# MLP of a two-layer decoder trunk: one buffer pool for both products, stepped weight loads, scratch split by group, last four groups by token tile

## The chip, the cores and the metric

One NeuronCore of a Trainium2 chip runs the whole program. The metric is the device time of one execution in microseconds (us); lower is better. Engines are named as in the profile: PE is TensorE, DVE VectorE, ACT ScalarE, POOL GpSimd, SP the engine whose queue issues nearly all DMAs.

## The reference, cut to what matters

Two layers over 1024 tokens of width 1024. Layer 0 mixes tokens with a causal pooling mixer, layer 1 with a gated DeltaNet; both then run the same MLP, whose two products are what the change is about (D = 1024, hidden width 4096):

```
x  = layer_norm(ALPHA * x + mix, ...)
ff = square(relu(x @ w1)) @ w2
pe = sigmoid(x @ gate_w + gate_b) * (p @ ple_proj)
x  = layer_norm(ALPHA * x + ff + pe, ...)
```

## The kernel before, in words

A float32 product is made of three float32r products: `split` (L66) rounds an operand to a high part (ACT copy, L68) and subtracts it for a low part (DVE, L69), and `mm3` (L71) issues high·high (L73), high·low (L74) and low·high (L75), each a 128x128 by 128x512 matmul.

Both MLP products are cut in 2x2 blocks and formed by seven block products instead of eight (P1 to P7, in the order P1, P2, P5, P6, P7, P4, P3 of the second product), whose operands are sums and differences of blocks. `mlp(i, ...)` (L306) runs once per layer i, in two stages:

**Stage A, h = square(relu(x @ w1))** (L325 to L419). The hidden width is taken in 16 pairs p of 128-column strips. A table `order` interleaves the products of pair p with the last two (P4, P3) of pair p-1, seven products of 12 matmuls a pair; `prep_a` prepares the weights three products ahead, from two loads of 512 KB into the three `raw` buffers. `multiply_a` evicts: the four blocks of h of the pair are c11, c12, c22, c21, and the combinations that the second product needs are hs2, hs3, hs4. All seven are 128x512 tiles from a pool `mlpa` of 10 buffers, made after P3 (L399 to L405: a DVE add, two ACT operations, four DVE operations) and stored by seven DMAs (L407) into one DRAM scratch tensor `h_d` for both layers.

**Stage B, ff = h @ w2** (L421 to L524). The pool of stage A is closed and a pool `mlpb` of five 128x2x512 buffers is opened. For each of seven products there are eight groups g; group g contracts over the strips of pairs 2g and 2g+1. `prep_b(k, g)` loads the left operand from `h_d` (L459, 512 KB into a `raw` buffer) and splits it into lh, ll (buffers `wh`, `wl` of a pool with two each); the right operand, a piece of w2, is split into rh, rl (pool `mlpb`). Sums of w2 blocks are formed in place by DVE (L323). `multiply_b` runs the group over four token tiles tt (24 matmuls a group, 192 a product, 1344 for all seven). w2 comes in 16 pieces of 1 MB through `load_w2` (L425): eight before the first group, eight when group 4 of P1 is reached (L507). The `big` pool of ten 16 KB-per-partition buffers holds them and, in stage A, the left operands r1.

The first four token tiles are normalised (`norm`, L495) after groups 1 to 4 of P3, one each; the last two groups of P3 run token tile by token tile, each followed by its `norm`. In layer 1 `layer_norm` (L101) writes the output by DMA (L126).

The order of instructions on each engine is fixed when the program is built, by a scheduler that places operations by readiness; within an engine, and on SP's queue, nothing overtakes. A tile that takes over a buffer waits for what last wrote or read it.

Of the kernel before, what the change touches and what calls it, by code (L numbers as in the profile page):

```python
# [7 lines left out]
F32 = mybir.dt.float32  # L8
# [24 lines left out]
def trunk(ctx: ExitStack, tc: tile.TileContext, io: dict):  # L33
# [272 lines left out]
    def mlp(i, r1, acc, row, finish=None, lag=0, out=None):  # L306
# [15 lines left out]
        stats = new_stats()  # L322
        sub = lambda o, a, b: V.tensor_tensor(o, a, b, ALU.subtract)  # L323
        add = lambda o, a, b: V.tensor_tensor(o, a, b, ALU.add)  # L324
        with tc.tile_pool(name=f"mlpa{i}", bufs=1) as q:  # L325
            new_h = lambda s: q.tile([P, 512], F32, tag="h", name=nm(s), bufs=10)
            st = {}
            n_op = [0]

# [34 lines left out]
            def multiply_a(p, k):  # L364
                d = st[p]
                o, ps, h = d["op"].pop(k), d["ps"], d["h"]
                bank = {P1: 0, P6: 0, P7: 0, P4: 0, P2: 1, P5: 2, P3: 2}[k]
                new = k in (P1, P2, P5)
                if new:
                    ps[bank] = new_ps()  # L370
                b = ps[bank]
                for kk in range(4):
                    mm3(b, o[:, 0, kk, :], o[:, 1, kk, :], r1[k][0][:, kk, :], r1[k][1][:, kk, :],
                        new and kk == 0, kk == 3, not new)

                def square(t):
                    A.activation(t, t, AF.Relu)
                    A.activation(t, t, AF.Square)

                if k == P1:  # L380
                    h[11] = new_h("c11")
                    A.copy(h[11], b)
                elif k == P2:
                    add(h[11], b, h[11])
                    square(h[11])
                elif k == P6:
                    h[12] = new_h("c12")
                    A.copy(h[12], b)
                elif k == P7:
                    h[22] = new_h("c22")  # L390
                    A.copy(h[22], b)
                    add(h[22], ps[2], h[22])
                    square(h[22])
                elif k == P4:
                    h[21] = new_h("c21")
                    A.activation(h[21], b, AF.Relu)
                    A.activation(h[21], h[21], AF.Square)
                elif k == P3:
                    add(h[12], b, h[12])  # L399
                    square(h[12])  # L400
                    s2, s3, s4 = (new_h(s) for s in ("hs2", "hs3", "hs4"))
                    sub(s3, h[12], h[11])
                    add(h[11], h[11], h[21])
                    sub(s2, h[11], h[12])
                    sub(s4, h[22], s2)  # L405
                    for n, t in ((P1, h[12]), (P2, h[22]), (P5, h[11]), (P6, s2), (P7, s3), (P4, h[21]), (P3, s4)):
                        nc.sync.dma_start(h_d[i, n, :, p, :], t)  # L407
                    del st[p]

            order = []  # L410
# [7 lines left out]
                    prep_a(*order[n + 3])  # L418
                multiply_a(*o)  # L419

        with tc.tile_pool(name=f"mlpb{i}", bufs=1) as q:  # L421
            new_op = lambda s, tag: (wsm if tag else q).tile([P, 2, 512], F32R, tag=tag or "op", name=nm(s), bufs=None if tag else 5)
            w = {}

            def load_w2(f, c):  # L425
                for e in range(2):
                    t = w[f, c, e] = new_big(F32, "w2").rearrange("p (g c) -> p g c", g=8)
                    src = io["w2"][i].rearrange("(g f p) c -> f p g c", f=2, p=P)
                    for b in range(2):
                        g = slice(e * 8 + b * 4, e * 8 + b * 4 + 4)  # L430
                        nc.sync.dma_start(t[:, b * 4:b * 4 + 4, :], src[f][:, g, cols(c)])

            def quad(f, c, g):
                return w[f, c, g // 4][:, g % 4 * 2:g % 4 * 2 + 2, :]

            ops = {}

            def prep_b(k, g):
                b11, b12, b21, b22 = ((f, c, 0) in w and quad(f, c, g) for f, c in ((0, 0), (0, 1), (1, 0), (1, 1)))
# [22 lines left out]
                split(rh, rl, r)  # L462
                ops[k, g] = lh, ll, rh, rl

            chain = {}
# [14 lines left out]
            def multiply_b(k, gs, tt):  # L480
                new = k in (P1, P2, P5)
                if new and gs[0] == 0:
                    chain[bank[k], tt] = new_ps()
                o = slice(tt * P, (tt + 1) * P)
                for g in gs:
                    lh, ll, rh, rl = ops[k, g]
                    for j in range(2):
                        mm3(chain[bank[k], tt], lh[:, j, o], ll[:, j, o], rh[:, j, :], rl[:, j, :],
                            new and g == 0 and j == 0, g == 7 and j == 1, not new)
                if gs[-1] == 7:  # L490
                    take(k, tt)
# [7 lines left out]
                if len(left) > lag:  # L499
                    left.pop(0)()  # L500

            load_w2(0, 0)
            load_w2(1, 0)
            seq = [(k, g) for k in (P1, P2, P5, P6, P7, P4, P3) for g in range(8)]
            prep_b(*seq[0])
            for n, (k, g) in enumerate(seq):
                if (k, g) == (P1, 4):  # L507
                    load_w2(0, 1)
                    load_w2(1, 1)
                if (k, g) == (P3, 0):  # L510
                    gb = new_big(F32, "gb")
                    g2, b2 = gb[:, 0:D], gb[:, D:2 * D]
# [1 line left out]
                    nc.sync.dma_start(b2, io["rows"][row + 4].partition_broadcast(P))  # L514
                if n + 1 < len(seq):
                    prep_b(*seq[n + 1])
                if (k, g) == (P3, 6):
                    continue
                for tt in range(4):
                    multiply_b(k, (6, 7) if (k, g) == (P3, 7) else (g,), tt)  # L520
                    if (k, g) == (P3, 7):
                        norm(4 + tt)
                if k == P3 and g in (1, 2, 3, 4):
                    norm(g - 1)  # L524
        return left

    x2_d = dram.tile([S, D], F32, name="x2_d")
# [706 lines left out]
```

## Time and profile before

| | |
|---|---|
| median of 3 runs | 2220.64 us (2218.31 to 2222.47) |
| the profiled execution's own time | 2214.46 us |
| its span, first to last instruction | 2212.7 us |
| mean granted TensorE clock | 0.985 |
| PE busy | 2136.8 us (97%), 10322 matmuls |
| DVE busy | 1523.7 us (69%) |
| ACT busy | 1058.6 us (48%) |
| DMA | 301.00 MB, mean 136 GB/s |

The page gives busy time by engine, the span in 40 slices, and the chain of work that ended last. The trace behind it can be asked for stretches of the span (`windows`), for single instructions in order of time (`timeline`) and for what each wait was ended by. In the timeline a row is: start in us, duration in us, engine, line, operation, tile written <- tiles read, shape, count, and in brackets the idle time of the engine just before, with what ended it. Tiles of one name in the program share a short name there: c11 to c22 are c, hs2 to hs4 are hs.

### The profile page before, as it was taken

To read this page: it belongs to the slowest core of one execution; us is meant where nothing else is said; L and a number is where in the kernel's file an instruction comes from. 1 tells how busy PE (TensorE), PEld (TensorE's weight loads), DVE (VectorE), ACT (ScalarE), POOL (GpSimd) and SP (SyncE) were. 2 spreads that over 40 slices of the span, in tenths; PEclk is the share of its full clock that TensorE was granted. 3 is DMA by queue.
4 is the path that set the end of the run, shared out by engine and by line. 5 is a ranking of instruction groups with operands and counts; after the bars stand their busy time and mean duration, and the time that the engine had idled before them with its cause. 6 is when DMAs were issued, how large, how long until landed. Compare 5 with 4: busy or idle time off the path is not lost.

```text
span 2212.7 us, 27931 instructions
## 1 busy us (share of the span) xinstructions
PE 2136.8 (97%) x10322; PEld 1784.3 (81%) x10322; DVE 1523.7 (69%) x2566; ACT 1058.6 (48%) x1814; POOL 24.4 (1%) x85
## 2 busy tenths in 40 slices
PE   7999999988999999999999999999999998899997
PEld 6887888866888878888887998888788887688886
DVE  7895666657674586879975677489666665657457
ACT  5434555543333456643455666343455554333334
POOL 0000000000000000000001000000000000000000
PEclk9999999998999999999999999999999999899999
DMA  8324445477333342341234445312444447733323
GB/s 297 110 81 138 153 157 153 146 246 262 102 114 96 96 144 84 92 128 48 91 129 127 117 129 183 122 35 84 135 157 149 149 149 245 270 96 115 98 92 124
DMA packets 158221, 301.00 MB, mean 136 GB/s; under 512 B 41410, under 2 KB 55106, under 8 KB 157764
## 3 DMA queue, kind: packets, MB, share of 16 engines
q1 hardware_dynamic: 153476, 290.82, 40.7%
q10 hardware_dynamic: 4608, 8.39, 1.0%
q8 instruction: 81, 1.33, 0.3%
q14 instruction: 56, 0.46, 0.1%
HBM read 208.99 MB, written 90.18 MB: 135 GB/s over the span
## 4 chain that ended last, share of the span: by engine, by line
PE 88%; DVE 6%; DMA 3%; ACT 2%; issue 1%; SPq 0%; DVEq 0%; ACTq 0%
PE ps L75 26%; PE ps L73 26%; PE ps L74 26%; DMA raw<-in_gate 1%; DVE w L323 1%; PE ps L134 1%; PE ps L772 1%; DMA raw<-in_w 1%; PE ps L746 1%; PE ps L1020 1%; PE ps L1042 1%; PE ps L984 1%; DMA stage<-in_pool_w 0%; PE ps L1008 0%; PE ps L1013 0%
## 5 line engine op out<-in xcount | busy, mean ns | idle before, releaser
L73 PE MATMUL ps<-rh,lh 128*128 128x512 f32 x896 | 351.9, 393 | 26.5 <-ACT rh L68 20.5
L75 PE MATMUL ps<-rh,ll 128*128 128x512 f32 x896 | 351.5, 392 | 9.0 <-DVE ll L69 9.0
L74 PE MATMUL ps<-rl,lh 128*128 128x512 f32 x896 | 351.3, 392 | 0.1
L69 DVE TENSOR_TENSOR rl<-w,rh 128x1024 fp32r<-128x1024 f32 x112 | 137.0, 1225 | 222.8 <-issue 174.3
L68 ACT CAST lh<-raw 128x1024 fp32r<-128x1024 f32 x112 | 118.1, 1055 | 353.6 <-PE ps L74 342.7
L73 PEld LDWEIGHTS ps<-rh,lh 128*128 128x128 f32 x896 | 169.7, 190 | 62.9 <-ACT rh L68 21.4
L75 PEld LDWEIGHTS ps<-rh,ll 128*128 128x128 f32 x896 | 169.8, 190 | 46.0 <-DVE ll L69 10.5
L73 PE MATMUL ps<-xh,wh 128*128 128x512 f32 x512 | 203.4, 397 | 1.2 <-ACT wh L68 1.2
L73 PE MATMUL ps<-xh,wo 128*128 128x512 f32 x512 | 200.3, 391 | 2.9 <-ACT wo L68 1.5
L75 PE MATMUL ps<-xh,wl 128*128 128x512 f32 x512 | 200.4, 391 | 1.1 <-DVE wl L69 1.1
L74 PE MATMUL ps<-xl,wh 128*128 128x512 f32 x512 | 200.1, 391 | 0.0
L74 PE MATMUL ps<-xl,wo 128*128 128x512 f32 x512 | 199.9, 390 | 0.0
L75 PE MATMUL ps<-xh,wo 128*128 128x512 f32 x512 | 199.8, 390 | 0.0
L74 PEld LDWEIGHTS ps<-rl,lh 128*128 128x128 f32 x896 | 169.8, 190 | 36.5 <-DVE rl L69 1.5
L69 DVE TENSOR_TENSOR wo<-raw,wo 128x512 fp32r<-128x512 f32 x192 | 132.3, 689 | 80.6 <-ACT wo L68 80.6
L68 ACT CAST wo<-raw 128x512 fp32r<-128x512 f32 x192 | 119.2, 621 | 104.4 <-PE ps L75 91.2
L73 PE MATMUL ps<-xt,wo 128*128 128x512 f32 x384 | 149.6, 390 | 2.1 <-ACT wo L68 2.1
L74 PE MATMUL ps<-xt,wo 128*128 128x512 f32 x384 | 149.4, 389 | 0.0
L75 PE MATMUL ps<-xt,wo 128*128 128x512 f32 x384 | 149.0, 389 | 0.0
L69 DVE TENSOR_TENSOR ll<-raw,lh 128x1024 fp32r<-128x1024 f32 x112 | 136.5, 1220 | 5.9 <-ACT lh L68 5.8
L68 ACT CAST rh<-w 128x1024 fp32r<-128x1024 f32 x112 | 116.8, 1046 | 30.3 <-PE ps L75 16.1
L324 DVE TENSOR_TENSOR c<-ps,c 128x512 f32<-128x512 f32 x96 | 66.1, 689 | 82.5 <-PE ps L75 73.9
(302 smaller groups left out, 4158.1 us busy)
## 6 DMA issues: line engine op xcount, KB each, us to landing
raw<-h_d SPq DMA_DIRECT2D x112, 512.0 KB, 3.5
raw<-in_w SPq DMA_DIRECT2D x64, 512.0 KB, 4.1
w<-in_w SPq DMA_DIRECT2D x32, 1024.0 KB, 8.2
h_d<-c SPq DMA_DIRECT2D x128, 256.0 KB, 2.1
h_d<-hs SPq DMA_DIRECT2D x96, 256.0 KB, 4.1
raw<-in_w_in SPq DMA_DIRECT2D x41, 512.0 KB, 3.5
pp_d<-tmp ACTq DMA_DIRECT2D x32, 256.0 KB, 3.1
raw<-in_gate SPq DMA_DIRECT2D x16, 512.0 KB, 4.9
```

What stands on the lines that cost most here:

```text
L68: A.copy(hi, src)
L69: V.tensor_tensor(lo, src, hi.bitcast(F32), ALU.subtract)
L73: T.matmul(ps, lh, rh, start=first, stop=False, skip_group_check=more)
L74: T.matmul(ps, lh, rl, start=False, stop=False, skip_group_check=more)
L75: T.matmul(ps, ll, rh, start=False, stop=last, skip_group_check=more)
L134: T.transpose(pss[q][:, j, :], y[:, k * P:(k + 1) * P], ident)
L323: sub = lambda o, a, b: V.tensor_tensor(o, a, b, ALU.subtract)
L324: add = lambda o, a, b: V.tensor_tensor(o, a, b, ALU.add)
L746: T.transpose(ps[:, j, :], chunk(tiles, half * 4 + j, h), ident)
L772: T.matmul(ps[:, j, :], kc, kc, start=True, stop=True)
L984: T.matmul(pq[:, j, :], hc("K", n, h), hc("Q", n, h), start=True, stop=True)
L1020: T.matmul(pv[:, j, :], d["X"][:, h, :], d["c"][:, 2 + gi, j], start=True, stop=True)
```

## The change

The seven single tiles of a pair become four paired ones ("c1" = c11 and c12, "c2" = c22 and c21, "hs23", and "hs4", of which half is used), from one pool `mlp` of five 128x2x512 buffers that stage B goes on using for rh and rl. The scratch is one DRAM tensor per layer and group of two pairs. A pair is stored by four DMAs (512, 512, 512 and 256 KB). The rl of the very first group of stage B is two single tiles from the pool `tmp`. `load_w2` loads one 1 MB piece a call: four before the first group, then one at every second group. The norms of the first four token tiles of P3 are asked for one group earlier in the code. In layer 1 (`out` is given) the last four groups of P3 run by token tile, with lh, ll, rh, rl in four `big` buffers; in layer 0 it stays at two groups.

```diff
-        with tc.tile_pool(name=f"mlpa{i}", bufs=1) as q:
-            new_h = lambda s: q.tile([P, 512], F32, tag="h", name=nm(s), bufs=10)
+        with tc.tile_pool(name=f"mlp{i}", bufs=5) as q:
+            new_h = lambda s: q.tile([P, 2, 512], F32, tag="q", name=nm(s))
+            place = {P5: 0, P1: 1, P2: 2, P4: 3, P6: 4, P7: 5, P3: 6}
...
-                    h[11] = new_h("c11")
+                    h[1] = new_h("c1")
+                    h[11], h[12] = h[1][:, 0], h[1][:, 1]
...
-                    h[22] = new_h("c22")
+                    h[2] = new_h("c2")
+                    h[22], h[21] = h[2][:, 0], h[2][:, 1]
...
-                    s2, s3, s4 = (new_h(s) for s in ("hs2", "hs3", "hs4"))
+                    d23, d4 = new_h("hs23"), new_h("hs4")
+                    s2, s3, s4 = d23[:, 0], d23[:, 1], d4[:, 0]
...
-                    for n, t in ((P1, h[12]), (P2, h[22]), (P5, h[11]), (P6, s2), (P7, s3), (P4, h[21]), (P3, s4)):
-                        nc.sync.dma_start(h_d[i, n, :, p, :], t)
+                    dst = h_d[i][p // 2][:, :, p % 2, :].rearrange("n p c -> p n c")
+                    nc.sync.dma_start(dst[:, 0:2], h[1])
+                    nc.sync.dma_start(dst[:, 2:4], h[2])
+                    nc.sync.dma_start(dst[:, 4:6], d23)
+                    nc.sync.dma_start(dst[:, 6], s4)
...
-        with tc.tile_pool(name=f"mlpb{i}", bufs=1) as q:
-            new_op = lambda s, tag: (wsm if tag else q).tile([P, 2, 512], F32R, tag=tag or "op", name=nm(s), bufs=None if tag else 5)
+            new_op = lambda s, tag: (wsm if tag else q).tile([P, 2, 512], F32R, tag=tag or "q", name=nm(s))
...
+            def load_w2(n):
+                f, c, e, b = n // 4 % 2, n // 8, n // 2 % 2, n % 2
...
+            g0 = 6 if out is None else 4
...
-                nc.sync.dma_start(l, h_d[i, k, :, 2 * g:2 * g + 2, :])
-                lh, ll, rh, rl = new_op("lh", "wh"), new_op("ll", "wl"), new_op("rh", None), new_op("rl", None)
+                nc.sync.dma_start(l, h_d[i][g][place[k]])
+                if k == P3 and g >= g0 and out is not None:
+                    if g == g0:
+                        tail.extend(new_big(F32R, s).rearrange("p (j c) -> p j c", j=8) for s in ("lh", "ll", "rh", "rl"))
+                    lh, ll, rh, rl = (z[:, 2 * (g - g0):2 * (g - g0) + 2, :] for z in tail)
+                elif k == P1 and g == 0:
+                    lh, ll, rh = new_op("lh", "wh"), new_op("ll", "wl"), new_op("rh", None)
+                    rl = None
...
+                if rl is None:
+                    A.copy(rh, r)
+                    rl = [new_tmp(F32R, "rl") for _ in range(2)]
+                    for j in range(2):
+                        V.tensor_tensor(rl[j], r[:, j], rh[:, j].bitcast(F32), ALU.subtract)
...
-            load_w2(0, 0)
-            load_w2(1, 0)
+            for n in range(4):
+                load_w2(n)
...
-                if (k, g) == (P1, 4):
-                    load_w2(0, 1)
-                    load_w2(1, 1)
+                if n % 2 == 0 and 4 + n // 2 < 16:
+                    load_w2(4 + n // 2)
...
-                if (k, g) == (P3, 6):
+                if k == P3 and 0 < g < 4:
+                    norm(g - 1)
+                if k == P3 and g == 4:
+                    norm(3)
+                if k == P3 and g0 <= g < 7:
                     continue
...
-                    multiply_b(k, (6, 7) if (k, g) == (P3, 7) else (g,), tt)
+                    multiply_b(k, range(g0, 8) if last else (g,), tt)
...
-    h_d = dram.tile([2, 7, P, 16, 512], F32, name="h_d")
+    h_d = [[dram.tile([7, P, 2, 512], F32, name=f"h{i}_{g}_d", tag=f"h{i}_{g}_d") for g in range(8)] for i in range(2)]
```

How the instructions stand on their engines, at the three places that matter. "waits" names what an instruction is made to wait for; DMAHW0 to DMAHW7 are eight counters that landed DMAs raise, which the DMAs use in turn.

ACT, layer 0, from the last pair's P3 into stage B, before: the relu and square of c12 (the last of stage A), then the casts for groups 0, 1 and 2.

```order
L377 ACTIVATE c12_519_3926<-c12_519_3926 128x512 [waits DVE_49]
L378 ACTIVATE c12_519_3926<-c12_519_3926 128x512 [waits Activation_49]
L68 CAST rh_534_4026<-w2_527_4010 128x1024 [waits DMAHW3_49,DMAHW4_49,DMAHW2_49,DMAHW5_49,DMAHW1_49,DMAHW6_49,DMAHW0_49,DMAHW7_49,DVE_49,Activation_49]
L68 CAST rh_539_4036<-w2_527_4010 128x1024
L68 CAST lh_537_4034<-raw_536_4032 128x1024 [waits DMAHW6_49,PE_49]
```

And with the change, the same place:

```order
L399 ACTIVATE c2_476_3881<-c2_476_3881 128x512 [waits Activation_49]
L68 CAST lh_489_3947<-raw_488_3945 128x1024 [waits DMAHW7_49,PE_49]
L379 ACTIVATE c1_465_3766<-c1_465_3766 128x512 [waits DVE_49]
L380 ACTIVATE c1_465_3766<-c1_465_3766 128x512 [waits Activation_49]
L480 CAST rh_484_3935<-w2_479_3925 128x1024 [waits DMAHW5_49]
L68 CAST rh_491_3949<-w2_479_3925 128x1024 [waits DMAHW0_49,DVE_49]
```

The first rh still stands behind the relu and the square, but waits for one counter in place of eight; the lh of group 1 has moved ahead of the two.

SP's queue, layer 0, first groups of stage B, before: the loads of groups 1 to 3, the pieces of w2, and the load of group 4 (`h_d_82` is the scratch).

```order
L459 DMA raw_536_4032<-h_d_82 128x1024 [waits DMAHW6_49]
L459 DMA raw_545_4070<-h_d_82 128x1024 [waits DMAHW7_49]
L459 DMA raw_550_4104<-h_d_82 128x1024 [waits DMAHW0_49]
L431 DMA w2_560_4172<-in_w2 128x4x512 [waits DMAHW1_49,PE_49]
L459 DMA raw_555_4138<-h_d_82 128x1024 [waits DMAHW6_49,DMAHW2_49,DVE_49]
L431 DMA w2_560_4172<-in_w2 128x4x512 [waits DMAHW3_49]
L431 DMA w2_561_4175<-in_w2 128x4x512 [waits DMAHW4_49,PE_49]
L431 DMA w2_561_4175<-in_w2 128x4x512 [waits DMAHW5_49]
L431 DMA w2_562_4178<-in_w2 128x4x512 [waits PE_49]
L431 DMA w2_562_4178<-in_w2 128x4x512 [waits DMAHW7_49]
L431 DMA w2_563_4181<-in_w2 128x4x512 [waits DMAHW0_49,PE_49]
L431 DMA w2_563_4181<-in_w2 128x4x512 [waits DMAHW1_49]
```

With the change, from the last pair's store of c2 on (`h0_7_d` is group 7 of layer 0's scratch):

```order
L411 DMA h0_7_d_89<-c2_476_3881 128x2x512 [waits DMAHW0_49,Activation_49]
L468 DMA raw_497_3983<-h0_2_d_84 128x1024 [waits DMAHW1_49]
L437 DMA w2_487_3943<-in_w2 128x4x512 [waits DMAHW2_49]
L410 DMA h0_7_d_89<-c1_465_3766 128x2x512 [waits DMAHW3_49,DVE_49,Activation_49]
L412 DMA h0_7_d_89<-hs23_477_3915 128x2x512 [waits DMAHW4_49,DVE_49]
L413 DMA h0_7_d_89<-hs4_478_3916 128x512 [waits DMAHW5_49,DVE_49]
L468 DMA raw_502_4018<-h0_3_d_85 128x1024 [waits DMAHW6_49]
L468 DMA raw_507_4052<-h0_4_d_86 128x1024 [waits DMAHW7_49]
L437 DMA w2_512_4086<-in_w2 128x4x512 [waits DMAHW0_49,PE_49]
L468 DMA raw_513_4088<-h0_5_d_87 128x1024 [waits DMAHW1_49,DVE_49]
L437 DMA w2_512_4086<-in_w2 128x4x512 [waits DMAHW2_49]
```

The loads of groups 2 to 5 now stand between single pieces of w2, and a piece of w2 stands ahead of the last pair's stores of c1, hs23 and hs4.

DVE, layer 1, the last token tile's norm, before (L474 takes the finished product into acc, L108 and L125 are the norm's wide operations; short ones between are left out):

```order
L108 SCALAR_TENSOR_TENSOR raw_2417_17260<-acc_1561_11049,lnsm_1782_12785,gb_2368_16911 128x1024
L474 SCALAR_TENSOR_TENSOR acc_1561_11049,lnsm_1782_12785<-ps_2212_15804,acc_1561_11049 128x512
L108 SCALAR_TENSOR_TENSOR raw_2419_17288<-acc_1561_11049,lnsm_1782_12785,gb_2368_16911 128x1024
L125 SCALAR_TENSOR_TENSOR acc_1561_11049<-raw_2417_17260,lnsm_1782_12785,gb_2368_16911 128x512 x2
L125 SCALAR_TENSOR_TENSOR acc_1561_11049<-raw_2419_17288,lnsm_1782_12785,gb_2368_16911 128x512 x2
```

And with the change:

```order
L108 SCALAR_TENSOR_TENSOR raw_2311_17055<-acc_1514_10966,lnsm_1735_12702,gb_2274_16730 128x1024
L125 SCALAR_TENSOR_TENSOR acc_1514_10966<-raw_2311_17055,lnsm_1735_12702,gb_2274_16730 128x512 x2
L498 SCALAR_TENSOR_TENSOR acc_1514_10966,lnsm_1735_12702<-ps_2117_15619,acc_1514_10966 128x512
L108 SCALAR_TENSOR_TENSOR raw_2313_17095<-acc_1514_10966,lnsm_1735_12702,gb_2274_16730 128x1024
L125 SCALAR_TENSOR_TENSOR acc_1514_10966<-raw_2313_17095,lnsm_1735_12702,gb_2274_16730 128x512 x2
```

The last tile's take and norm stand behind a finished third norm. On PE the matmuls of token tiles 0 and 1 of the last four groups are interleaved; those of tiles 2 and 3 (24 each) follow one after the other.

## Rows read from the trace of the kernel before

**Rows 1.** The page, chain that ended last, whole span

```profile
PE 88%; DVE 6%; DMA 3%; ACT 2%; issue 1%; SPq 0%; DVEq 0%; ACTq 0%
```

**Rows 2.** Windows: busy us (count) of PE, PEld, DVE, ACT, POOL; PEclk, DMA share, GB/s

```profile
480.00:500.00 20.00, 8.97 (x37) 6.46 (x35) 6.37 (x8) 7.25 (x11) 0.00 (x0) 0.81 0.98 344
...
560.00:580.00 20.00, 20.00 (x90) 16.57 (x89) 9.17 (x8) 7.68 (x8) 0.00 (x0) 1.00 0.30 86
```

**Rows 3.** Timeline, PE, both layers' first product of stage B: after a gap

```profile
499.03 1.22 PE L73 MATMUL ps<-rh,lh 128*128 128x512 f32 x2 [10.35 <-ACT rh L68]
...
531.78 0.50 PE L73 MATMUL ps<-rh,lh 128*128 128x512 f32 x1 [3.38 <-ACT lh L68]
...
536.61 0.79 PE L75 MATMUL ps<-rh,ll 128*128 128x512 f32 x1 [4.09 <-DVE ll L69]
...
1884.15 1.22 PE L73 MATMUL ps<-rh,lh 128*128 128x512 f32 x2 [10.16 <-ACT rh L68]
...
1916.46 0.50 PE L73 MATMUL ps<-rh,lh 128*128 128x512 f32 x1 [2.62 <-ACT lh L68]
...
1922.06 0.79 PE L75 MATMUL ps<-rh,ll 128*128 128x512 f32 x1 [4.86 <-DVE ll L69]
```

**Rows 4.** Timeline, DVE and ACT, layer 0, end of stage A

```profile
488.71 0.69 DVE L324 TENSOR_TENSOR c<-ps,c 128x512 f32<-128x512 f32 x1 [3.62 <-PE ps L75]
489.44 0.63 ACT L377 ACTIVATE c<-c 128x512 f32<-128x512 f32 x1 [2.18 <-DVE c L324]
...
492.94 0.69 DVE L323 TENSOR_TENSOR hs<-c,hs 128x512 f32<-128x512 f32 x1
...
497.93 2.94 ACT L68 CAST rh<-w 128x1024 fp32r<-128x1024 f32 x3 [7.20 <-DMA h_d<-hs]
```

**Rows 5.** Timeline, SP's queue, layer 0, groups 3 to 8 of stage B

```profile
506.80 10.64 SPq L431 DMA_DIRECT2D w<-in_w  x7
517.53 20.50 SPq L459 DMA_DIRECT2D raw<-h_d  x5
```

**Rows 6.** Timeline, DVE, layer 0, the second gap

```profile
529.65 5.76 DVE L323 TENSOR_TENSOR w<-w,w 128x1024 f32<-128x1024 f32 x5
535.33 2.36 DVE L69 TENSOR_TENSOR ll<-raw,lh 128x1024 fp32r<-128x1024 f32 x2
```

**Rows 7.** Timeline, PE, start of stage A in layer 0: slow matmuls after short gaps

```profile
184.30 0.50 PE L73 MATMUL ps<-xt,wo 128*128 128x512 f32 x1 [1.05 <-ACT wo L68]
...
185.16 0.63 PE L73 MATMUL ps<-xh,wo 128*128 128x512 f32 x1
...
188.15 0.57 PE L74 MATMUL ps<-xl,wo 128*128 128x512 f32 x1
```

**Rows 8.** Tile view of the scratch h_d, all its DMAs

```profile
DMA to landing us min/median/max: 2.0/3.4/13.1
```

**Rows 9.** The page, groups: a DVE subtract from SBUF, 128x512

```profile
L69 DVE TENSOR_TENSOR wo<-raw,wo 128x512 fp32r<-128x512 f32 x192 | 132.3, 689 | 80.6 <-ACT wo L68 80.6
```

**Rows 10.** Timeline, DVE and ACT, stage A, one pair's evictions after its P3

```profile
474.15 0.69 DVE L324 TENSOR_TENSOR c<-ps,c 128x512 f32<-128x512 f32 x1 [1.37 <-PE ps L75]
...
476.93 0.69 DVE L324 TENSOR_TENSOR c<-c,c 128x512 f32<-128x512 f32 x1
...
478.86 0.69 DVE L323 TENSOR_TENSOR hs<-c,hs 128x512 f32<-128x512 f32 x1
...
482.31 0.58 ACT L391 COPY c<-ps 128x512 f32<-128x512 f32 x1 [4.33 <-PE ps L75]
```

**Rows 11.** Timeline, PE and DVE, layer 1, the end of the program

```profile
2194.43 0.39 PE L73 MATMUL ps<-rh,lh 128*128 128x512 f32 x1
...
2201.01 0.39 PE L75 MATMUL ps<-rh,ll 128*128 128x512 f32 x1
...
2203.47 0.68 DVE L474 SCALAR_TENSOR_TENSOR acc<-ps,acc 128x512 f32<-128x512 f32 x1
...
2207.88 1.41 DVE L125 SCALAR_TENSOR_TENSOR acc<-raw,lnsm,gb 128x512 f32<-128x512 f32 x2
```

More of the change, by code (lines that the diff above doesn't have):

```diff
@@ L394, in multiply_a @@
                 elif k == P4:
-                    h[21] = new_h("c21")
                     A.activation(h[21], b, AF.Relu)
@@ L419, in mlp @@
                 multiply_a(*o)
-        with tc.tile_pool(name=f"mlpb{i}", bufs=1) as q:
-            new_op = lambda s, tag: (wsm if tag else q).tile([P, 2, 512], F32R, tag=tag or "op", name=nm(s), bufs=None if tag else 5)
+            new_op = lambda s, tag: (wsm if tag else q).tile([P, 2, 512], F32R, tag=tag or "q", name=nm(s))
             w = {}
[L425 to L431, printed above, removed]
+            def load_w2(n):
+                f, c, e, b = n // 4 % 2, n // 8, n // 2 % 2, n % 2
+                if not b:
+                    w[f, c, e] = new_big(F32, "w2").rearrange("p (g c) -> p g c", g=8)
+                src = io["w2"][i].rearrange("(g f p) c -> f p g c", f=2, p=P)
+                g = slice(e * 8 + b * 4, e * 8 + b * 4 + 4)
+                nc.sync.dma_start(w[f, c, e][:, b * 4:b * 4 + 4, :], src[f][:, g, cols(c)])
             def quad(f, c, g):
@@ L436, in mlp @@
             ops = {}
+            tail = []
+            g0 = 6 if out is None else 4
             def prep_b(k, g):
-                b11, b12, b21, b22 = ((f, c, 0) in w and quad(f, c, g) for f, c in ((0, 0), (0, 1), (1, 0), (1, 1)))
+                b11, b12, b21, b22 = ((f, c, g // 4) in w and quad(f, c, g) for f, c in ((0, 0), (0, 1), (1, 0), (1, 1)))
                 if k == P1:
@@ L458, in prep_b @@
                 l = new_raw().rearrange("p (j c) -> p j c", j=2)
-                nc.sync.dma_start(l, h_d[i, k, :, 2 * g:2 * g + 2, :])
-                lh, ll, rh, rl = new_op("lh", "wh"), new_op("ll", "wl"), new_op("rh", None), new_op("rl", None)
-                split(lh, ll, l)
-                split(rh, rl, r)
+                nc.sync.dma_start(l, h_d[i][g][place[k]])
[6 more added lines that the diff above has]
+                    rl = None
+                else:
+                    lh, ll, rh, rl = new_op("lh", "wh"), new_op("ll", "wl"), new_op("rh", None), new_op("rl", None)
+                split(lh, ll, l)
+                if rl is None:
[3 more added lines that the diff above has]
+                        V.tensor_tensor(rl[j], r[:, j], rh[:, j].bitcast(F32), ALU.subtract)
+                else:
+                    split(rh, rl, r)
+                    rl = [rl[:, j] for j in range(2)]
                 ops[k, g] = lh, ll, rh, rl
@@ L487, in multiply_b @@
                     for j in range(2):
-                        mm3(chain[bank[k], tt], lh[:, j, o], ll[:, j, o], rh[:, j, :], rl[:, j, :],
+                        mm3(chain[bank[k], tt], lh[:, j, o], ll[:, j, o], rh[:, j, :], rl[j],
                             new and g == 0 and j == 0, g == 7 and j == 1, not new)
@@ L516, in mlp @@
                     prep_b(*seq[n + 1])
-                if (k, g) == (P3, 6):
+                if k == P3 and 0 < g < 4:
[3 more added lines that the diff above has]
+                if k == P3 and g0 <= g < 7:
                     continue
+                last = (k, g) == (P3, 7)
                 for tt in range(4):
-                    multiply_b(k, (6, 7) if (k, g) == (P3, 7) else (g,), tt)
-                    if (k, g) == (P3, 7):
+                    multiply_b(k, range(g0, 8) if last else (g,), tt)
+                    if last:
                         norm(4 + tt)
-                if k == P3 and g in (1, 2, 3, 4):
-                    norm(g - 1)
         return left
```

1 line of the change is left out of this document (removed).

## The prediction, made before the changed kernel ran

> **What bounds the kernel now.** I read the chain of waits first: 88% of the span is PE [rows 1], so time is won only where PE stands still or runs slowly. The windows say where. Twenty us well inside stage B hold 90 matmuls at a granted clock of 1.00; the twenty us at its start hold 37, at 0.81, while the DMA engines are 0.98 busy [rows 2]. The same matmuls run at other places, so the start of stage B is the place that the change works on. PE's timeline there shows two gaps in each layer: 10.35 and 10.16 us before the first matmul, and some 30 us later a pair of 3.38 + 4.09 and 2.62 + 4.86 us [rows 3].
>
> What ends them: the first ends with ACT's cast of the first rh. ACT itself had been idle for 7.20 us, and what it waited for was a DMA from an hs tile to the scratch [rows 4]: `mlpb` takes over the room of `mlpa`, so its first tile waits until all stores of stage A have landed. The second ends with lh and then ll. On SP seven pieces of w2 are issued in a row, from 506.80 for 10.64 us, and the loads of the next groups follow only after them [rows 5]; and DVE makes five in-place w sums, 5.76 us, just ahead of the late ll [rows 6].
>
> **What stage B loses.** At the end of layer 1 matmuls start 29 apart from 2194.43 to 2201.01 [rows 11], 0.2269 us each. The 1344 of a stage B need 304.9 us at that pace. In layer 1 PE falls idle at 1884.15 - 10.16 = 1873.99 [rows 3] and ends its last matmul at 2201.40 [rows 11]: 327.4 us, a loss of 22.5. Of it 17.6 is idle in the three gaps; the other 4.9 are slow matmuls after them. Layer 0 has gaps of 17.8, and I take the same 22.5.
>
> **The first gap, after.** I work it out in layer 0. PE ends P3 of the last pair at 499.03 - 10.35 = 488.68. ACT now has the lh cast of group 1 first. It waits for that PE end for its buffer, and from three casts in 2.94 us [rows 4] I take 1.0 us: 489.7. Then relu and square, 0.63 each [rows 4]: 491.0. Then the first rh, 1.05 with what lies between: 492.05, when PE does one matmul and needs rl. DVE meanwhile does add c (end 489.4), the ll of group 1 (half of 2.36 [rows 6], say 1.2), then its four operations on c and hs, which start 0.73 apart (last from 490.76 to 492.94 before [rows 4]): 493.9. The rl is two subtractions, and PE needs only the first, 0.69 [rows 9]: 494.6. So PE is idle 3.4 us and, but for one matmul, 2.5 more: 494.6 - 488.7 - 0.2 = 5.7.
>
> After it the matmuls start slowly. In stage A a gap of 1.05 us is followed by eight matmuls that start 0.43 us apart, against 0.23 [rows 7]: 8 x 0.2 = 1.6 us. I charge that to the new gap: 7.3 us in all. For the ground between, the whole 4.9 of slow matmuls stays if the gap is still enough (loss 10.6) and none if it isn't (5.7); 1.6 is the nearest row, since 5.7 us is in two pieces and one gap replaces two. Gain 22.5 - 7.3 = **15.2 us a layer** (bounds 11.9 and 16.8).
>
> **The second gap, after.** I cost it at nothing. A piece of w2 now follows every second group, so SP never has more than one between two group loads. One group takes 24 x 0.2269 = 5.45 us on PE. DVE has per group an ll and an rl (1.2 each) and per two groups one or two w sums of 1.15 (5.76 / 5): under 4.9 us of the 5.45. The DMA need of a group is 0.5 MB and half a piece, 1.0 MB; at 344 GB/s [rows 2] that is 3.1 us. If that cover is thin somewhere, the price is the second rival's. The groups at risk are 1 and 2, whose operands are the last pair's and the stores around it: the rl of group 1 takes the buffer of the last c1, whose store is issued at about 492.5, and with a landing of 3.4 us [rows 8] it can be cast and subtracted by 498; PE needs it at 494.6 + 5.45 + 1.6 - 0.3 = 501.3.
>
> **Stage A.** Five buffers of two halves replace ten singles. Two waits are new. The ACT copy that writes the first half of c2 needs the hs4 subtraction of the pair before: that ends at 479.55, and the copy starts at 482.31 [rows 10], 2.8 us spare. Behind it on ACT are the casts of a later product, which PE wants only products later. And the ACT copies that open c1 and c2 take buffers of earlier pairs and wait for their stores. In the tighter case such a store can go some 3.4 us after its pair's P3 (after relu, square and the operations on hs), and the buffer is needed four products, 4 x 12 x 0.2269 = 10.9 us, after that P3, so 7.5 us are there for a landing whose median is 3.4 and whose worst in this trace is 13.1 [rows 8]. I take zero: the median lies well inside. The worst is kept for the rival on the slow side. The 512 KB stores may land later than the 256 KB ones of before; in turn SP issues four stores a pair for seven, 96 fewer in all, and waits for their data anyway: zero.
>
> **The tail, layer 1.** Before, PE ends at 2201.40, the last take begins at 2203.47, 2.07 us late, because DVE is still on the tile before, and L125 ends at 2209.29; the span ends at 2212.7, 11.3 us after PE. After, the last four groups run by tile. Tiles 0 and 1 are interleaved on PE and end about 12.5 and 10.9 us before PE's end E (two tiles of 24 matmuls, 5.45 each, lie behind). A chain is the one of before, from the last tile's place in DVE's queue to the end of L125, under 4.8 us; DVE does two by E - 3.9 (8.6 us from E - 12.5, they overlap a little), and the third, 4.8 us, by E + 0.9. The last tile's take then starts at E + 0.9, and L125 ends at E + 5.6, and with the 3.4 us that lie between the last L125 and the end of the span before, the end is E + 9.0 in place of E + 11.3: **gain 2.3 us**. Bounds: -1, where ll of group 7 comes late (it is ready about 1 us ahead by my count) or DVE takes longer with the two chains; +3.1, where the last take doesn't wait at all. I take the count. In layer 0 the norms asked for one group earlier are DVE work under a P3 that still has PE running: zero.
>
> **The sum.** 2 x 15.2 + 2.3 = 32.7 us. The profiled execution's own time is 2214.46, which gives 2181.8. That execution lies 0.28% under the median of the three runs, 2220.64, and under their fastest; scaled by 1.0028, the forecast for a median is **2188 us**. A change of 0.2%, 4.4 us, is about what a measurement of this kernel can tell from none.
>
> **The rivals.** (1) *The clock stays up.* Against my 1.6: after the 2.62 us gap of layer 1 the next matmul took 0.50 us [rows 3], as short as one at speed with its fill, and no slow run follows. If the two short pieces of the new gap don't lower the clock, 2 x 1.6 more: 2185. For it speaks that row, against it the slow matmuls after a gap of 1.05 us [rows 7]. [...] 10%.
>
> (2) *Stores queue behind a piece of w2.* With the change a piece of w2 stands on SP ahead of the last pair's stores of c1, hs23 and hs4. A piece at 344 GB/s is 3.0 us, and the DMA engines are 0.98 busy there already [rows 2]. If the c1 store needs the worst landing seen, 13.1 us [rows 8], the rl of group 1 is ready at 492.5 + 13.1 + 1.2 = 506.8 against 501.3: 5.5 us, and 1.6 of slow matmuls, 7 a layer: 2188 + 14 = 2202. The median of 3.4 is against it, that this is the most crowded stretch of the program for it. The Trainium skill ("DMA: Bandwidth & Descriptors", the paragraph on HWDGE ordering) says that each DMA engine takes descriptors of one issuing engine in ring order, which speaks against this change: a store waits its turn behind the piece; no row here shows the order within a queue. 15%.
>
> (3) *The change doesn't do what it says.* The first rh still comes as late as before (it again waits in effect for the last stores, or its load of w2 is late); only the second gap goes, 7.5 us of idle and half of the slow matmuls, 9.9 a layer: 2 x 9.9 + 2.3 = 22, own time 2192.4, median 2198.5. Against it: the row of the first rh in the order names one counter for eight. 8%.
>
> (4) *Slower.* Fewer, larger buffers make stage A wait. If the larger stores land in more than 7.5 us, ACT's evictions into c1, and PE behind it for its PSUM tile, wait in each of some 28 pairs (32 without the first two of each layer). From 32.7 / 28 = 1.2 us a pair, a landing of 8.7 us, this decides; at 10 us it is 28 x 2.5 = 70, so 37 slower: 2258. For it is only the worst landing, against it the median and that a pair of stage A moves its bytes over 19 us (84 x 0.2269), not in the crowd of [rows 2]. 3%.
>
> **How the numbers follow.** My forecast has 64%, with 2181 to 2194 of its own (from the bounds: 2 x 1.6 better; 2 x 3.3 worse, tail 3 worse, not all at once). With rivals 1 and 2 most of the chance lies within 2179 to 2203, which I give as the range; it takes in rival 3 too, and leaves out rival 4 and sums of several misses. All but rival 4, and a small remainder around no change, are faster by over 0.2%: faster 0.94, same 0.03, slower 0.03.
>
> **What would show it.** PE's first gap of stage B falls from over 10 us to about 3.4, and a second of 2.5 follows after one matmul, ended by DVE's rl; ACT's first rh no longer waits on a DMA from an hs tile. No gap over 1 us in the 50 us behind it; one there ended by a DMA of c or hs, or by a cast of the group 1 or 2 operands, is rival 2. Stage A's pairs keep their length; ACT copies into c1 that wait on a DMA to the scratch are rival 4. From PE's last matmul to the end of the span there should be 9, not 11.3 us. I am wrong if the gaps shrink and the time doesn't follow them, or if the first rl is late for something other than DVE's queue.

## The result, and the profile after

The changed kernel takes 2186.61 us (median of 4 runs, 2185.44 to 2188.05), the kernel before, on the same chip, 2219.47 (4 runs, 2214.88 to 2222.47): a ratio of 0.9854 with an interval of 0.9835 to 0.9873. The forecast was 2188.

Both profiled executions can be cut at the same four places, read from PE's timeline. A length is the difference of two ends of matmuls or starts.

| stretch | before, us | after, us |
|---|---|---|
| stage B of layer 0, from PE's last matmul of stage A | 331.7 | 317.8 |
| stage B of layer 1, likewise | 327.4 | 313.6 |
| from PE's last matmul to the end of the span | 11.3 | 8.1 |
| all the rest | 1542.3 | 1545.5 |
| span | 2212.7 | 2185.0 |

Stage B gains 13.9 and 13.8 us, the tail 3.2: 30.9. The rest is 3.2 longer, and 2.4 of that lie between the end of stage B of layer 0 and the start of stage A of layer 1. No kernel here changes the code there, and yet the ten profiles of this study lie between 745.5 (the kernel before) and 748.7 us in that stretch. Up to 3 us there thus come and go without any edit; with one profile a kernel it is not shown that they are scatter from run to run.

PE's gaps in the changed kernel, from the timeline; they answer to [rows 3]. The columns are those of the rows ahead of the prediction.

```profile
491.65 0.76 PE L73 MATMUL ps<-rh,lh 128*128 128x512 f32 x1 [3.73 <-issue]
494.18 0.79 PE L74 MATMUL ps<-rl,lh 128*128 128x512 f32 x1 [1.76 <-DVE rl L483]
494.77 0.63 PE L75 MATMUL ps<-rh,ll 128*128 128x512 f32 x1
...
498.18 0.49 PE L74 MATMUL ps<-rl,lh 128*128 128x512 f32 x1
...
1866.72 0.49 PE L73 MATMUL ps<-rh,lh 128*128 128x512 f32 x1 [3.43 <-ACT rh L480]
1869.29 0.79 PE L74 MATMUL ps<-rl,lh 128*128 128x512 f32 x1 [2.08 <-DVE rl L483]
...
2158.69 0.50 PE L73 MATMUL ps<-rh,lh 128*128 128x512 f32 x1 [0.43 <-ACT lh L68]
```

The 10 us gap has become 3.7 + 1.8, with one matmul between, and the gaps 32 to 37 us further in are gone. From 494.77 to 498.18 eight matmuls start 0.43 us apart: the slow stretch that the forecast charged. The granted clock from 494.1 to 498.5 is 0.51, the lower of its two levels (1.2 and 2.4 GHz). What releases the start, on ACT, DVE and SP of the same stretch ([rows 4] before):

```profile
487.96 0.69 DVE L324 TENSOR_TENSOR c<-ps,c 128x512 f32<-128x512 f32 x1 [3.62 <-PE ps L75]
488.38 1.04 ACT L68 CAST lh<-raw 128x1024 fp32r<-128x1024 f32 x1 [1.88 <-DMA raw<-h_d]
...
489.99 0.63 ACT L380 ACTIVATE c<-c 128x512 f32<-128x512 f32 x1
490.52 1.03 ACT L480 CAST rh<-w 128x1024 fp32r<-128x1024 f32 x1
...
492.13 0.36 SPq L410 DMA_DIRECT2D h_d<-c  x1
...
492.83 0.69 DVE L323 TENSOR_TENSOR hs<-c,hs 128x512 f32<-128x512 f32 x1
493.44 1.28 DVE L483 TENSOR_TENSOR rl<-w,rh 128x512 fp32r<-128x512 f32 x2
...
495.68 1.22 DVE L69 TENSOR_TENSOR rl<-w,rh 128x1024 fp32r<-128x1024 f32 x1 [0.96 <-DMA h_d<-c]
```

The first rh is cast at 490.52 with no idle time in front of it: it waits for its place on ACT, no longer for a store. The rl comes behind the last hs on DVE. The last line is the rl of group 1: the store of c1, issued at 492.13, has landed by 495.68. The windows at the start of stage B, and 22 us later (columns as in [rows 2]):

```profile
488.00:510.00 22.00, 16.58 (x62) 13.22 (x63) 11.85 (x13) 9.24 (x10) 0.00 (x0) 0.84 0.96 329
510.00:540.00 30.00, 30.00 (x134) 24.85 (x133) 26.14 (x25) 10.48 (x11) 0.00 (x0) 1.00 0.94 345
```

PE is never idle in the second one, but the DMA engines are 0.94 busy in it. The end of the program, answering to [rows 11]:

```profile
2175.91 1.41 DVE L125 SCALAR_TENSOR_TENSOR acc<-raw,lnsm,gb 128x512 f32<-128x512 f32 x2
...
2176.52 0.39 PE L75 MATMUL ps<-rh,ll 128*128 128x512 f32 x1
...
2177.25 0.68 DVE L498 SCALAR_TENSOR_TENSOR acc<-ps,acc 128x512 f32<-128x512 f32 x1
...
2180.57 1.41 DVE L125 SCALAR_TENSOR_TENSOR acc<-raw,lnsm,gb 128x512 f32<-128x512 f32 x2
```

The last take follows PE's end, 2176.91, by 0.34 us in place of 2.07. It comes straight behind the third tile's L125 (2175.91 to 2177.32).

### The profile page after: what moved, and what is told of

Its sections match the earlier page's. It is cut to its first block, busy times and chain, and to the rows that moved or that the text cites. A ratio compares the mean times of both kernels' runs of the same rounds, so it can differ in the third digit from the quotient of the medians.

```text
span 2185.0 us, 27693 instructions
## 1 busy us (share of the span) xinstructions
PE 2136.6 (98%) x10322; PEld 1786.3 (82%) x10322; DVE 1526.5 (70%) x2568; ACT 1064.7 (49%) x1814; POOL 24.2 (1%) x85
## 4 chain that ended last, share of the span: by engine, by line
PE 87%; DVE 6%; DMA 3%; ACT 2%; issue 1%; SPq 0%; ACTq 0%; DVEq 0%
PE ps L75 26%; PE ps L74 26%; PE ps L73 26%; DMA raw<-in_gate 1%; DMA raw<-h_d 1%; PE ps L134 1%; PE ps L798 1%; PE ps L772 1%; DMA raw<-in_w 1%; PE ps L1046 1%; PE ps L1068 1%; PE ps L1010 1%; PE ps L1034 1%; DMA stage<-in_pool_w 0%; PE ps L1039 0%
```

## The experiments

All kernels below were timed against the kernel before, in three rounds or more. "Stage B" gives layer 0 and layer 1, cut as in the table above (before 331.7 and 327.4, after 317.8 and 313.6); about 305 us of it are its matmuls at speed, and in layer 0 some 5 us more are transposes of finished token tiles on PE, in every kernel. With the first four kernels the kernel before had a median of 2217.99 us, with the last four 2217.03, and with the changed kernel 2219.47; so a difference between two medians below is uncertain by some 2 us.

| kernel | median, us | ratio to before | stage B, us |
|---|---|---|---|
| changed, two pools | 2197.02 | 0.9905 [0.9883, 0.9926] | 323.7, 320.0 |
| changed, w2 in two batches | 2215.81 | 0.9992 [0.9981, 1.0002] | 333.1, 329.2 |
| changed, tail of two groups | 2188.10 | 0.9861 [0.9844, 0.9878] | 317.5, 312.7 |
| changed, early operands | 2170.36 | 0.9782 [0.9765, 0.9798] | 310.7, 305.4 |
| before, stepped loads alone | 2197.61 | 0.9906 [0.9884, 0.9928] | 323.3, 318.5 |
| changed, first eight pieces at once | 2200.75 | 0.9918 [0.9893, 0.9943] | 325.3, 321.5 |
| early operands, w2 in two batches | 2216.45 | 0.9996 [0.9986, 1.0007] | 333.1, 328.5 |
| changed, one scratch tensor | 2185.78 | 0.9851 [0.9830, 0.9872] | 317.4, 314.2 |

**Two pools.** The pool of stage B is opened anew.

```diff
             for n, o in enumerate(order):
...
+        with tc.tile_pool(name=f"mlpb{i}", bufs=5) as q:
             new_op = lambda s, tag: (wsm if tag else q).tile([P, 2, 512], F32R, tag=tag or "q", name=nm(s))
```

> The changed kernel, but stage B opens a pool of its own (five buffers of the same size) where stage A's pool has closed; stepped w2 loads, paired tiles, split scratch and the tail stay. Theory (room: the first gap was the wait of the first rh for all stores of stage A): the last store of hs4 is issued at 493.6 in the changed kernel's trace and lands some 3.5 us later, so the first rh is cast at 497 to 498 and PE starts in earnest at about 498.8 instead of 494.2: 4.6 us a layer, 9 us in all, about 2196. The gap in layer 0 is again about 10 us in one piece, and no second gap comes. Rival (crowd: the first gap shrank because fewer pieces of w2 are in flight there, the pool does nothing): no change, 2186 to 2188, first gap in two pieces as in the changed kernel.

10.4 us slower than the changed kernel by the medians, as the theory had it; by the profiles the two stages B are 5.9 and 6.3 us longer. PE's timeline and ACT's, in layer 0:

```profile
498.18 1.04 ACT L481 CAST rh<-w 128x1024 fp32r<-128x1024 f32 x1 [8.04 <-DMA h_d<-hs]
...
499.27 0.80 PE L73 MATMUL ps<-rh,lh 128*128 128x512 f32 x1 [12.03 <-ACT rh L481]
```

ACT sits idle for 8.04 us until a store of an hs tile has landed. The wait for room is the first gap; pairing, stepped loads and tail don't remove it. PE starts 12.0 us after stage A where I had worked out 498.8 - 487.9 = 10.9.

**w2 in two batches.** The loads as in the kernel before, in the changed kernel.

```diff
-            for n in range(4):
+            for n in range(8):
                 load_w2(n)
...
-                if n % 2 == 0 and 4 + n // 2 < 16:
-                    load_w2(4 + n // 2)
+                if (k, g) == (P1, 4):
+                    for m in range(8, 16):
+                        load_w2(m)
```

> The changed kernel, but w2 is loaded as before in two batches of eight pieces (before the first group and at group 4 of P1); one pool, split scratch and the tail stay. Theory (queue: the second gap was w2 pieces ahead of the group loads on SP): the gap of two pieces some 35 us into stage B comes back, 7.5 us a layer and about 2 of slow matmuls after it, less 1.0 at the first gap because the lh cast of group 1 no longer stands ahead of the first rh on ACT: 8 to 9 a layer, 17 in all, about 2203. The first gap stays under 6 us. Rival (crowd): the first gap grows back to about 10 us as well, 13 or more a layer, 2213 and up.

2215.81: nearly the whole gain is gone, 29.2 us, where my theory had 17. But the rival is not what happened either, since the first gap stayed short (timeline, PE and SP, layer 0):

```profile
490.12 0.77 PE L73 MATMUL ps<-rh,lh 128*128 128x512 f32 x1 [3.09 <-issue]
492.65 0.79 PE L74 MATMUL ps<-rl,lh 128*128 128x512 f32 x1 [1.76 <-DVE rl L483]
503.22 0.66 PE L73 MATMUL ps<-rh,lh 128*128 128x512 f32 x1 [3.25 <-ACT lh L68]
529.91 0.50 PE L73 MATMUL ps<-rh,lh 128*128 128x512 f32 x1 [2.74 <-ACT lh L68]
535.50 0.79 PE L75 MATMUL ps<-rh,ll 128*128 128x512 f32 x1 [4.87 <-DVE ll L69]
...
493.86 4.00 SPq L468 DMA_DIRECT2D raw<-h_d  x3
...
504.45 0.32 SPq L468 DMA_DIRECT2D raw<-h_d  x1
504.82 10.75 SPq L437 DMA_DIRECT2D w<-in_w  x7
515.67 21.26 SPq L468 DMA_DIRECT2D raw<-h_d  x5
```

Three stalls have taken the place of two: the start, one for the lh of group 1, whose load now goes out at 493.86 behind pieces of w2 (480.65 in the changed kernel), and the old second gap behind seven pieces on SP. Here stage A ends at 487.03, and the last of the stalls is over at 535.50, 48.5 us later. In the kernel before that was 536.61 - 488.68 = 47.9 [rows 3]. So PE, started earlier, waits at the same loads until the same time. Layer 1 gives 48.4 and 48.1 in the same way. That made a new theory: with w2 in batches the arrival of loads paces PE for the first 48 us, and what the pool wins at the start is given back.

**Tail of two groups.**

```diff
-            g0 = 6 if out is None else 4
+            g0 = 6
```

> The changed kernel, but the token-tile part of layer 1 covers the last two groups, as before and as in layer 0. Theory: from PE's last matmul to the end of the span 11.3 us as before, instead of 8.1; the rest as in the changed kernel: 3.2 us slower, about 2190. Rival (the end is set by the last tile's own chain and its output DMA whatever the number of groups): 8.1 us stays and the time is that of the changed kernel.

The tail of the profile grew to 2185.2 - 2174.55 = 10.65 us, 2.6 more. The median rose by 1.5, which is not clear of noise: the interval of its ratio overlaps that of the changed kernel. Direction as in the theory, the size a little less than the 3.2 of the profiles before and after. DVE's rows show why:

```profile
2174.16 0.39 PE L75 MATMUL ps<-rh,ll 128*128 128x512 f32 x1
...
2175.70 1.41 DVE L125 SCALAR_TENSOR_TENSOR acc<-raw,lnsm,gb 128x512 f32<-128x512 f32 x2
...
2178.79 1.41 DVE L125 SCALAR_TENSOR_TENSOR acc<-raw,lnsm,gb 128x512 f32<-128x512 f32 x2
2180.83 1.42 DVE L125 SCALAR_TENSOR_TENSOR acc<-raw,lnsm,gb 128x512 f32<-128x512 f32 x2
```

PE is done at 2174.55, and three tiles' L125 still lie behind that, not one.

**Early operands.** The first rh and rl and the second rh go to single tiles of the idle pool `tmp`; the second rl takes the pool buffer that this frees.

```diff
                 elif k == P1 and g == 0:
-                    lh, ll, rh = new_op("lh", "wh"), new_op("ll", "wl"), new_op("rh", None)
+                    lh, ll = new_op("lh", "wh"), new_op("ll", "wl")
+                    rh = [new_tmp(F32R, "rh") for _ in range(2)]
                     rl = None
+                elif k == P1 and g == 1:
+                    lh, ll, rl = new_op("lh", "wh"), new_op("ll", "wl"), new_op("rl", None)
+                    rh = [new_tmp(F32R, "rh") for _ in range(2)]
...
-                    A.copy(rh, r)
-                    rl = [new_tmp(F32R, "rl") for _ in range(2)]
-                    for j in range(2):
-                        V.tensor_tensor(rl[j], r[:, j], rh[:, j].bitcast(F32), ALU.subtract)
+                if k == P1 and g < 2:
+                    rl = [rl[:, j] for j in range(2)] if rl is not None else [new_tmp(F32R, "rl") for _ in range(2)]
+                    for j in range(2):
+                        split(rh[j], rl[j], r[:, j])
```

> The changed kernel, but rh and rl of the first group and rh of the second are single tiles of the pool tmp, which is idle there, so that they can be made before stage A ends, and the rl of the second group takes the buffer that the first rh had. Theory (room: what is left of the first gap is operands made after the last pair's h because of their buffers and their place on ACT and DVE): the gap falls from 3.7 + 1.8 us to under 1, group 1 is ready before group 0 ends, and the slow matmuls after the gap (ten, 2.0 us) go with it: 5 to 7.5 us a layer, 10 to 15 in all, 2172 to 2177. Rival (the lh and ll of the groups, or the load of h, set the start): the gap is ended by lh or ll and the time is within 3 us of 2186.6.

2170.36, 16.3 us faster than the changed kernel and 2.2% faster than before: a little over the theory's range. In layer 0 (timeline, PE) the first matmul of stage B follows the last of stage A at once:

```profile
484.98 0.39 PE L75 MATMUL ps<-xh,wo 128*128 128x512 f32 x1
485.21 0.39 PE L73 MATMUL ps<-rh,lh 128*128 128x512 f32 x1
...
492.46 0.47 PE L74 MATMUL ps<-rl,lh 128*128 128x512 f32 x1 [0.97 <-issue]
```

and the windows of the first 40 us show a full clock, with the slow stretch gone as well:

```profile
485.00:505.00 20.00, 19.03 (x84) 15.46 (x83) 12.81 (x14) 9.37 (x10) 0.00 (x0) 1.00 0.97 338
505.00:525.00 20.00, 20.00 (x89) 16.55 (x89) 12.49 (x12) 6.48 (x7) 0.00 (x0) 1.00 0.88 316
```

Stage B of layer 1 takes 305.4 us, all but the 304.9 that its matmuls need. What was left of the gap came from the first operands being made behind the last pair's h on ACT and DVE; whether their buffers or their places held them there, this run, which changes both, doesn't tell.

**Stepped loads alone**, in the kernel before.

```diff
-            load_w2(0, 0)
-            load_w2(1, 0)
+            for n in range(4):
+                load_w2(n)
...
-                if (k, g) == (P1, 4):
-                    load_w2(0, 1)
-                    load_w2(1, 1)
+                if n % 2 == 0 and 4 + n // 2 < 16:
+                    load_w2(4 + n // 2)
```

> The kernel before with the stepped loads of w2 alone; pools, single tiles, one scratch tensor and the tail are as before. Theory (the stepped loads carry most of the gain, the paired tiles and the split scratch none): the time of the changed kernel with two pools, 2197, plus the 2.6 us that the shorter tail is worth, 2199 to 2201; the first gap near 10 us, no second gap. Rival (paired stores and the split scratch are needed for the loads to come in time): a gap stays within 50 us of the start of stage B, and the time is over 2205.

2197.61, some 2 us better than expected. Stage B is as long as with two pools, within 1.5 us, so single tiles and one scratch cost nothing there. The steps carry 8.3 and 8.9 us of the gain by themselves. One gap is left in each layer (PE, timeline). The view puts its end down to a load of h, but ACT's row shows the wait of the kernel before again: the first rh is cast only when a store of an hs tile has landed, and PE starts as that cast ends, at 496.7.

```profile
496.74 1.22 PE L73 MATMUL ps<-rh,lh 128*128 128x512 f32 x2 [10.55 <-DMA raw<-h_d]
495.65 2.94 ACT L68 CAST rh<-w 128x1024 fp32r<-128x1024 f32 x3 [7.18 <-DMA h_d<-hs]
...
1875.87 1.22 PE L73 MATMUL ps<-rh,lh 128*128 128x512 f32 x2 [10.27 <-DMA raw<-h_d]
```

**First eight pieces at once**, the other eight in steps.

```diff
-            for n in range(4):
+            for n in range(8):
                 load_w2(n)
...
-                if n % 2 == 0 and 4 + n // 2 < 16:
-                    load_w2(4 + n // 2)
+                if n % 2 == 0 and 8 + n // 2 < 16:
+                    load_w2(8 + n // 2)
```

> The changed kernel, but eight pieces of w2 are loaded ahead of the first group and the other eight in steps, one at every second group. Theory (each stall belongs to the group loads that stand behind w2 pieces on SP): the load of group 1 stands behind three pieces and the last stores, so PE waits 2.5 to 3.5 us for the lh of group 1 as with two batches (3.25 and 2.38 + 0.53 there) and runs slowly after it, but the gap some 35 us into stage B does not come: 4 to 5 us a layer, 2195 to 2197. Rival (the second gap comes from DVE's sums of w2 blocks and from the bytes in flight, not from the order on SP): a gap of over 4 us is seen there too, and the time is over 2200.

2200.75, above the theory's 2197 and just into what the rival named, but by the profile the theory's places: one stall at group 1 and none later.

```profile
493.17 2.07 SPq L437 DMA_DIRECT2D w<-in_w  x2
495.30 1.20 SPq L468 DMA_DIRECT2D raw<-h_d  x2
...
506.06 0.80 PE L73 MATMUL ps<-rh,lh 128*128 128x512 f32 x1 [5.27 <-ACT lh L68]
...
527.44 3.48 DVE L323 TENSOR_TENSOR w<-w,w 128x1024 f32<-128x1024 f32 x3
```

The load of group 1 goes out at 495.30, right behind two pieces, where the changed kernel issues it at 480.65:

```profile
480.65 0.93 SPq L468 DMA_DIRECT2D raw<-h_d  x1
```

The stall is 5.27 us, not 3; that is what I had undersized. That stall lies with a load behind pieces on SP. The missing second gap says less against DVE's sums of w2 blocks than I had planned: with the pieces spread, the sums are spread too, at most three in a row here against five just ahead of the late ll before [rows 6].

**Early operands, w2 in two batches.** The edits of the two experiments together; their code is shown above.

> The kernel with early operands for the first two groups, but w2 in two batches of eight as before. Theory (given back: with the batches the arrival of the group loads sets the pace, so whatever PE gains at the start it waits for later): near the 2215.8 of the changed kernel with two batches, 2208 to 2218; stage B's first gap is gone and the gaps behind it are as much longer. Rival (gains add): 2215.8 - 16.2 = 2199.6.

2216.45: the 16 us that early operands win with stepped loads are worth nothing with batches. PE's timeline in layer 0, where stage A ends at 488.13 and PE goes straight on:

```profile
502.57 1.04 ACT L68 CAST lh<-raw 128x1024 fp32r<-128x1024 f32 x1 [3.51 <-DMA raw<-h_d]
503.67 0.79 PE L73 MATMUL ps<-rh,lh 128*128 128x512 f32 x1 [10.10 <-DMA raw<-h_d]
...
529.43 5.76 DVE L323 TENSOR_TENSOR w<-w,w 128x1024 f32<-128x1024 f32 x5
530.33 0.50 PE L73 MATMUL ps<-rh,lh 128*128 128x512 f32 x1 [2.29 <-ACT lh L68]
536.38 0.79 PE L75 MATMUL ps<-rh,ll 128*128 128x512 f32 x1 [5.31 <-DVE ll L69]
```

No gap at the start, and 10.10 us at group 1 instead; the last stall ends 48.3 us after stage A, as in the two kernels above (47.9 and 48.5) whose starts were 10 and 5 us later. The wait had only changed its place. This settles the new theory against the sum of gains. The first place is plain: the lh of group 1 is cast when its load has landed, 14.4 us after the end of stage A here, 15.1 with two batches alone (502.12) and 15.4 in the kernel before:

```profile
504.09 1.05 ACT L68 CAST lh<-raw 128x1024 fp32r<-128x1024 f32 x1 [3.22 <-DMA raw<-h_d]
```

The last stall is less plain. In all three kernels it is ended by an ll that stands on DVE behind five sums of w2 blocks, 5.76 us long. No run takes these sums away and leaves the batches, so how much of the last 4 to 5 us belongs to them and how much to the loads stays open.

**One scratch tensor.**

```diff
-                nc.sync.dma_start(l, h_d[i][g][place[k]])
+                nc.sync.dma_start(l, h_d[i, g, place[k]])
...
-                    dst = h_d[i][p // 2][:, :, p % 2, :].rearrange("n p c -> p n c")
+                    dst = h_d[i, p // 2][:, :, p % 2, :].rearrange("n p c -> p n c")
...
-    h_d = [[dram.tile([7, P, 2, 512], F32, name=f"h{i}_{g}_d", tag=f"h{i}_{g}_d") for g in range(8)] for i in range(2)]
+    h_d = dram.tile([2, 8, 7, P, 2, 512], F32, name="h_d")
```

> The changed kernel with one scratch tensor for both layers, indexed by layer and group, in place of sixteen. The order on the engines and on SP is the same, and so are the blocks that are stored and loaded. Theory (the split does nothing): 2185 to 2188. Rival (the split lets loads start sooner or changes how the stores land): over 2190.

2185.78, within the spread of the changed kernel: the split of the scratch is worth nothing here.

## Why the prediction was right, point by point

**The time.** 2188 was forecast, 2186.61 measured. Part of that closeness is luck. Worked from the profiled execution's own time the sum gave 2181.8, and the changed kernel's own is 2186.78: 5.0 us short of the forecast gain. Of these 2.7 are stage B (13.9 and 13.8 for 15.2 each), -0.9 the tail, and 3.2 all the rest, most of it outside the code that the change touches. The factor 1.0028 to the median stood in for the scatter; it was the right thing to do for a forecast of a median, since the profiled execution before lay under all three runs, but it also covered 2.7 us of my own.

**The first gap.** Right in mechanism and size: rh cast at 490.52 to 491.55, rl behind the last hs, a loss of 494.18 - 487.92 - 0.23 = 6.0 us in layer 0 against 5.7. Two pools bring the wait back. That the lh of group 1 had to wait for its load I had not seen. ACT stood idle for 1.88 us ahead of it, but all save the last 0.45 us of that was the wait for PE's end that I had counted.

**The slow matmuls.** Eight at 0.2 us, as charged, plus half a microsecond around the first ones: 2.1 in layer 0. Layer 1 has one or two more of them. With 0.43 us for the lh of a late group there, the loss of stage B in layer 1 is 313.6 - 304.9 = 8.7 where I had 7.3. This term was mis-sized; the mechanism held. Rival 1 (the clock stays up) fell in both layers.

**The second gap.** Gone, as forecast, but the step behind it was wrong in its count. I had a piece of w2 at every second group, never more than one between two group loads, and 1.0 MB in 5.45 us. In SP's timeline nearly every group load is followed by a piece, and some by two, since they stand on the queue ahead of their place in the code:

```profile
509.34 0.34 SPq L468 DMA_DIRECT2D raw<-h_d  x1
509.73 0.43 SPq L437 DMA_DIRECT2D w<-in_w  x1
514.78 0.34 SPq L468 DMA_DIRECT2D raw<-h_d  x1
515.17 0.43 SPq L437 DMA_DIRECT2D w<-in_w  x1
...
520.61 0.98 SPq L437 DMA_DIRECT2D w<-in_w  x2
```

So 1.5 MB and more go per group, 345 GB/s, and the cover is thin: the DMA engines are 0.94 busy for 30 us, and DVE is busy for 26.14 of them. That is 4.75 us a group, just inside my bound of 4.9, since it has two or three w sums a group where I had one or two in two groups. Four more pieces ahead of the loads cost 14 us over the two layers (the first eight at once, 2200.75 against 2186.61). Rival 2 named a neighbour of this mechanism, stores behind a piece, and it did not decide here: the store of c1 was down within 3.6 us. Loads behind pieces are what it missed, and they stall PE at group 1 in the three experiments with eight pieces at once. The rule of the Trainium skill that I set beside it ("DMA: Bandwidth & Descriptors", the paragraph on HWDGE ordering) agrees with these runs as far as they go: with the first eight pieces at once the load of group 1, issued at 495.30 behind more pieces, let ACT cast the lh only at 504.96, and in the changed kernel at 488.38. No run shows the order within the queue itself.

**How the parts add.** I had added the two gaps of a layer as if each could be removed alone. For the first gap that step was wrong. With the other edits in place the steps are worth 29.2 us and the pool 10.4; the steps without the pool still win 19.4 by the medians of those runs (2217.03 to 2197.61), but the pool and the tail without the steps only 2.2 (2217.99 to 2215.81), which its interval of 0.9981 to 1.0002 doesn't tell from nothing. The sum was right because both were made.

**Stage A.** No new wait. From its first matmul to its last, stage A takes 308.1 and 309.8 us in the two layers, against 309.8 and 308.2 before, so together they are as long as they were (617.9 and 618.0). ACT never idles ahead of the copies that open c1 (L385), and ahead of those that open c2 (L394) it waits for PE alone, 32 times; a wait of ACT for a store, the condition of rival 4, is not among them.

**The tail.** 8.1 us against the forecast 9.0. The take waits for the third tile's chain on DVE, as I had it, but that chain is over 0.34 us after PE's end and not 0.9; the last chain ends 5.1 us after PE, and 3.0 and not 3.4 lie behind that. Rival 3 (the change doesn't do what it says) fell with the first gap.

## What to carry to other kernels

When a stretch has several gaps, ask of each whether its end is set by PE's own progress or by the clock of something else, such as the arrival of loads: the time from the last common point to the end of the last gap is a hint (47.9, 48.5 and 48.3 us for three different starts), and the run with only the start moved is the test. In the second case an earlier start only moves the wait, and the loads have to be spread first. Once they are, the operands of a stage's first steps are worth a buffer that nobody else is using: two more pairs of small tiles in an idle pool, beside the one pair that the change had put there, gave half as much again as the whole change (16.3 us on top of 32.9).

## What the runs showed of the hardware

The same short gap of PE is followed by slow matmuls in one execution and not in the next. Each stage A has a gap of 1.05 us near its start. Behind it, in layer 0 of the kernel before [rows 7], eight matmuls ran 0.43 us apart, at a granted clock of 0.51 (185.1 to 188.6, the lower of the two levels). In the other nine profiles the matmuls at that place of layer 0 ran at full speed, 1.00 in the changed kernel; one of the nine, stepped loads alone, differs from the kernel before only in stage B. In layer 1 seven profiles have the slow run, the changed kernel's among them, and the kernel before and two others have not. That is 1.6 us that come and go. After every start of stage B with a gap of 3 us or more some matmuls ran slowly, in all eight profiles that have such a gap; in the two with early operands PE goes straight on, and with stepped loads its clock stays at 1.00 there.
